# Attention scores as pairs of 64-row matmuls, with queries and keys loaded once and query tiles taken two at a time

## The chip, the cores and the metric

One NeuronCore of a Trainium2 chip runs the whole program. Its engines work side by side, each on its own queue: PE (TensorE, matmuls, with its weight loads, PEld, beside them), DVE (VectorE), ACT (ScalarE), POOL (GpSimd) and SP (SyncE), of which SP and POOL also issue the DMA transfers. The metric is the device time of one execution in microseconds. Differences of about 1% are the smallest that a measurement of this kernel tells from no change.

## What is computed

A two-layer decoder step in fp32, for a prompt of 2048 tokens and 32 sample tokens. Each layer projects its input, runs a branch (a state-space scan in layer 0, windowed attention with ALiBi in layer 1), adds attention over 256 memory slots, gates both, projects back and normalises. The change touches the two attentions of the prompt. Cut to what matters:

```python
def mem_attention(q, mem_k, mem_v):              # 4 heads of 64, 256 memory slots, in both layers
    s = jnp.einsum('bthe,bmhe->bhtm', q, mem_k).astype(jnp.float32) * SCALE
    p = jax.nn.softmax(s, axis=-1)
    o = jnp.einsum('bhtm,bmhe->bthe', p.astype(mem_v.dtype), mem_v)

def _dilated_group_full(q, k, v, slopes, window, dil):   # 3 groups (128,1), (512,4), (2048,16), 4 heads each
    # inside each residue stream: blocks of n=128 queries against (previous block, current block) of keys
    s = jnp.einsum('brjihe,brjuhe->brjhiu', qb, kb).astype(f32) * SCALE + bias
    s = jnp.where(valid[:, None], s, NEG_INF)
    lse = jax.nn.logsumexp(s, axis=-1)
    p = jnp.exp(s - lse[..., None])
    o = jnp.einsum('brjhiu,brjuhe->brjihe', p.astype(vb.dtype), vb)
```

## The kernel before

Every fp32 matmul whose precision matters is made of fp32r parts: a value is split into a high and a low part (`split`, L121: the high part by ACT, the low one by DVE). A projection is three matmuls, high x high, high x low and low x high (`mm3`, L126 to L130). The projections fill PE nearly all the time; the rows of the profile show them as `mm<-XH,wh` and the like. `XH` and `XL` are the split input, loaded from DRAM through `xraw`; `wh`, `wl` and `v` are split weights.

Beside the projections runs a side chain, written as a Python generator. The main loop calls `tick` after each three matmuls; `tick` advances the generator by one step (up to its next `yield`) for every so much projection work (`self.R` holds the rates). So the side chain's instructions are laid between the projections' in the order of the program, and a scheduler that knows when operands will be there settles the order on each engine. The attentions are parts of this side chain: `mem_attention` once in layer 0 (at 480 to 610 us of the profiled execution) and once in layer 1 (957 to 1150 us), `dilated` three times in layer 1, once for each group (from 1195, 1425 and 1635 us), with `dil_sample` after each.

Both attentions work on tiles of 128 queries and on two heads at a time, in blocks of four tiles:

- `load` brings queries (and, in `dilated`, keys) of one block from DRAM by POOL's queue into `qraw` or `raw`. One buffer holds one head: its 64 rows are read twice, into both halves of the 128 partitions (the `[0, 2]` in the access pattern, L915, L1541, L1542).
- `prep` makes `qs`, whose upper 64 partitions hold the high part of the scaled queries and whose lower ones the low part (ACT L927 or L1559, then DVE on 64 partitions, L928 or L1560), and splits the keys into `kh` and `kl` on both halves. In the memory attention `KH` and `KL` are made once.
- `st1` makes the scores of one tile: for each head one matmul with `kh` and one with `kl`, over 128 rows that hold the high and the low part of the queries, into `s` in PSUM (L938 and L939, L1579 and L1580); `s` has two buffers. In `mem_attention` DVE takes the extremum (`nm`, L941), ACT the exponential out of `s` (L945), DVE and POOL scale by the inverse sum (L950). In `dilated` DVE adds the bias, writes `P` and takes the extremum (`st`, L1583), and ACT takes the exponential in place (L1585).
- `st2` transposes `P` on PE (L959, L1595), and ACT and DVE in turn copy the result out to `PT` (`copy_out`, L132).
- `st3` multiplies with the values into `o`, 64 columns of the array for each head (L971, L1609; each fp32 matmul is two instructions in the trace). After the fourth tile of a block `o` is copied out to `ct` or `oT` and the same buffer serves the next block.

A step of the generator holds `st1` of tile n, then, after the `yield`, `st3` of tile n-4 and `st2` of tile n-2. In `dilated` the first group has three buffers of `raw`, the others four, two of which make a block; `qraw` has four. Nine steps pass between the first loads and the first `prep` of a `dilated`.

Of the kernel before, what the change touches and what calls it, by code (L numbers as in the profile page):

```python
# [13 lines left out]
OP = mybir.AluOpType  # L14
# [45 lines left out]
class Trunk:  # L60
# [827 lines left out]
    def mem_attention(self, l, d, side):  # L888
# [3 lines left out]
        with self.pool("ma", side=side) as p, self.pool("maps", space=PSUM, side=side) as psum:  # L892
            KH = p.tile([128, 4, 256], F32R, name="KH")
            KL = p.tile([128, 4, 256], F32R, name="KL")
            V = p.tile([128, 2, 256], F32, name="V")
            self.q2.dma_start(V, d["mv"][l].rearrange("(m p) t -> p m t", p=128))
            kd = []
            for h in range(0, 4, 2):
                raw = p.tile([128, 512], F32, name="qraw", bufs=4)
                for x in range(2):  # L900
                    self.q2.dma_start(raw[x * 64:x * 64 + 64].rearrange("p (h t) -> p h t", h=2),
                                      d["mk"][l, h * 64:h * 64 + 128].rearrange("(h e) t -> e h t", e=64))
                kd.append(raw.rearrange("p (h t) -> p h t", h=2))
# [6 lines left out]
            def load(j):  # L910
                ht, c0 = at(j)
                raws[j] = []
                for h in range(2):
                    raw = p.tile([128, 512], F32, name="qraw", bufs=4)
                    self.q2.dma_start(raw, dview(d["mq"], (ht * 2 + h) * 64 * NT + c0, [[0, 2], [NT, 64], [1, 512]]))  # L915
                    raws[j].append(raw)
# [6 lines left out]
            def prep(j):  # L923
                QS[j] = []
                for raw in raws.pop(j):
                    qs = p.tile([128, 512], F32R, name="qs", bufs=4)
                    nc.scalar.activation(qs, raw, AF.Copy, scale=-0.125)  # L927
                    v.scalar_tensor_tensor(qs[64:128], raw[64:128], -0.125, qs[64:128].bitcast(F32),  # L928
                                           op0=OP.mult, op1=OP.subtract)
                    QS[j].append(qs)  # L930

            def st1(n):
                j, t = divmod(n, 4)
                ht = at(j)[0]
                ts = slice(t * 128, t * 128 + 128)
                s = psum.tile([128, 2, 256], F32, name="s", bufs=2)
                for h in range(2):
                    mm(s[:, h], QS[j][h][:, ts], KH[:, ht * 2 + h], start=True, stop=False)  # L938
                    mm(s[:, h], QS[j][h][:, ts], KL[:, ht * 2 + h], start=False, stop=True)  # L939
                nm = p.tile([128, 2], F32, name="nm", bufs=4)  # L940
                v.tensor_reduce(nm, s, axis=AX.X, op=OP.min)  # L941
                P = p.tile([128, 2, 256], F32, name="P", bufs=3)
                sm = p.tile([128, 2], F32, name="sm", bufs=4)
                for h in range(2):
                    nc.scalar.activation(P[:, h], s[:, h], AF.Exp, scale=-1.0, bias=nm[:, h:h + 1],  # L945
                                         accum_out=sm[:, h:h + 1])
                rs = p.tile([128, 2], F32, name="rs", bufs=4)
                v.reciprocal(rs, sm)
                for h, eng in enumerate((v, nc.gpsimd if l == 0 else v)):
                    eng.tensor_scalar(P[:, h], P[:, h], rs[:, h:h + 1], None, op0=OP.mult)  # L950
                PP[n] = P

            def st2(n):
                P = PP.pop(n)
                tp = psum.tile([128, 2, 2, 128], F32, name="tp", bufs=2)
                PT[n] = p.tile([128, 2, 2, 128], F32, name="PT", bufs=3)
                for h in range(2):
                    for k in range(2):
                        nc.tensor.transpose(tp[:, h, k], P[:, h, k * 128:k * 128 + 128], ident)  # L959
                self.copy_out(PT[n], tp)  # L960

            def st3(n):
                j, t = divmod(n, 4)
# [3 lines left out]
                o, pt = O[j], PT.pop(n)  # L967
                for k in range(2):
                    for h in range(2):
                        c = (ht * 2 + h) * 64  # L970
                        mm(o[h * 64:h * 64 + 64, t * 128:t * 128 + 128], V[:, k, c:c + 64], pt[:, h, k],  # L971
                           start=k == 0, stop=k == 1)
                if t < 3:
                    return
# [8 lines left out]
            for h in range(2):  # L983
                self.split(KH[:, h * 2:h * 2 + 2], KL[:, h * 2:h * 2 + 2], kd[h])
            load(1)
            yield
# [3 lines left out]
            for n in range(36):  # L990
                if l == 0 and n == 8:
                    yield from self.wait("mg0")
                if n < 32:
                    st1(n)
                if n % 4 == 0 and n < 24:
                    load(n // 4 + 2)
                if l == 0 and n % 4 == 0 and n < 32:
                    load_gate(n // 4)
                if n % 4 == 2 and n < 28:
                    prep(n // 4 + 1)  # L1000
                yield
                if n >= 4:
                    st3(n - 4)
# [1157 lines left out]
```

## Time and profile before

| | us |
|---|---|
| median of 3 runs | 2058.67 |
| lowest and highest | 2046.83, 2061.18 |
| the profiled execution | 2061.28 |
| its span, first to last instruction | 2059.5 |

The profile is of one execution. An engine's busy time says how long it worked, and its idle time is put down to what ended it. A matmul's duration in the trace is from its issue to its modelled end; matmuls are pipelined, so that the distance from one start to the next, not the duration, is what one costs PE. PE's clock is given as the share of full speed that was granted in a stretch.

### The profile page before, as it was taken

The numbers are of one execution on the slowest core, as the hardware profiler recorded it, in microseconds if no ns is written. First come the engines' busy times: TensorE is split into PE (matmuls) and PEld (weight loads), VectorE is DVE, ScalarE is ACT, GpSimd is POOL, SyncE is SP. The second block draws the span as 40 slices with busy tenths as digits, with TensorE's granted clock in tenths as the row PEclk, the third lists the DMA queues.
The fourth block names the chain that finished last, engine by engine and source line by source line (L and its number), as shares of the span: only waits on it lengthen the run. The fifth ranks groups of instructions, "written<-read, shape, count | busy, mean of one in ns | idle before, by whom it ended". The sixth has DMA issues, their size and how long they took to land.

```text
span 2059.5 us, 35000 instructions
## 1 busy us (share of the span) xinstructions
PE 1943.8 (94%) x12806; PEld 1652.1 (80%) x12806; DVE 1235.8 (60%) x2888; ACT 722.7 (35%) x1651; POOL 490.5 (24%) x824
## 2 busy tenths in 40 slices
PE   8999999899899999998999988998899989999998
PEld 6789888788789887877888877797778767888777
DVE  8649989875676666663665146523652256454675
ACT  5333222424553311142454136522661256231010
POOL 0414444215430022211100122022302321311220
PEclk9999999999999999999999999999999989999999
DMA  7685655657659899876443496638958876858951
GB/s 223 188 225 139 186 176 178 207 167 224 179 161 271 281 347 368 293 237 174 117 142 100 143 197 172 165 101 189 208 148 234 200 166 188 274 167 246 278 164 72
DMA packets 473381, 406.56 MB, mean 197 GB/s; under 512 B 158264, under 2 KB 414696, under 8 KB 469928
## 3 DMA queue, kind: packets, MB, share of 16 engines
q1 hardware_dynamic: 384472, 257.52, 44.3%
q0 software_dynamic: 88736, 146.79, 24.0%
q8 instruction: 101, 1.65, 0.3%
q14 instruction: 72, 0.59, 0.1%
HBM read 297.99 MB, written 150.27 MB: 218 GB/s over the span
## 4 chain that ended last, share of the span: by engine, by line
PE 63%; DMA 19%; DVE 7%; issue 4%; ACT 2%; SPq 2%; POOL 2%; DVEq 0%; POOLq 0%; ACTq 0%
PE mm L128 17%; PE mm L129 16%; PE mm L130 16%; DMA raw<-e_kT 4%; DMA ot<-e_oT 2%; PE o L971 2%; DMA bcraw<-in_ssm_bc 2%; PE tp L959 2%; PE o L1609 2%; PE tp L1595 1%; DMA xraw<-d_x1TB 1%; DMA xraw<-in_xT 1%; DMA wraw<-in_w_in 1%; DMA xraw<-d_x1TA 1%; DMA wraw<-in_w_kv 1%
## 5 line engine op out<-in xcount | busy, mean ns | idle before, releaser
L128 PE MATMUL mm<-XH,wh 128*128 128x512 f32 (+2 forms) x1520 | 547.2, 361 | 23.9 <-DVE us L1391 8.3
L129 PE MATMUL mm<-XH,wl 128*128 128x512 f32 (+2 forms) x1520 | 543.3, 358 | 1.0 <-DVE wl L124 1.0
L130 PE MATMUL mm<-XL,wh 128*128 128x512 f32 (+2 forms) x1520 | 542.3, 358 | 1.4 <-DVE XL L124 1.4
L128 PEld LDWEIGHTS mm<-XH,wh 128*128 128x128 f32 x1520 | 290.2, 191 | 65.7 <-DVE us L1391 8.5
L130 PEld LDWEIGHTS mm<-XL,wh 128*128 128x128 f32 x1520 | 290.1, 191 | 43.2 <-DVE XL L124 2.9
L129 PEld LDWEIGHTS mm<-XH,wl 128*128 128x128 f32 x1520 | 289.6, 191 | 39.4 <-issue 2.6
L129 PE MATMUL mm<-WOH,cl 128*128 128x512 f32 (+1 forms) x512 | 198.6, 388 | 7.4 <-DVE cl L124 7.4
L128 PE MATMUL mm<-WOH,ch 128*128 128x512 f32 (+1 forms) x512 | 200.0, 392 | 0.4 <-ACT ch L123 0.4
L130 PE MATMUL mm<-WOL,ch 128*128 128x512 f32 (+1 forms) x512 | 198.7, 388 | 0.0
L124 DVE TENSOR_TENSOR XL<-xraw,XH 128x512 fp32r<-128x512 f32 (+2 forms) x176 | 99.7, 595 | 60.7 <-ACT XH L123 60.5
L124 DVE TENSOR_TENSOR wl<-wraw,wh 128x1024 fp32r<-128x1024 f32 (+1 forms) x87 | 103.6, 1191 | 48.6 <-ACT wh L123 47.8
L123 ACT ACTIVATE XH<-xraw 128x512 fp32r<-128x512 f32 (+2 forms) x176 | 92.5, 553 | 82.0 <-DMA xraw<-d_x1TB 27.3
L129 PEld LDWEIGHTS mm<-WOH,cl 128*128 128x128 f32 x512 | 96.8, 189 | 29.6 <-DVE cl L124 9.3
L128 PE MATMUL mm<-v,XH 128*128 128x256 f32 (+1 forms) x408 | 117.9, 289 | 0.2 <-DVE s L138 0.2
L130 PE MATMUL mm<-v,XH 128*128 128x256 f32 (+1 forms) x408 | 116.2, 285 | 0.0
L129 PE MATMUL mm<-v,XL 128*128 128x256 f32 (+1 forms) x408 | 116.0, 284 | 0.0
L130 PEld LDWEIGHTS mm<-WOL,ch 128*128 128x128 f32 x512 | 96.8, 189 | 21.3
L128 PEld LDWEIGHTS mm<-WOH,ch 128*128 128x128 f32 x512 | 96.6, 189 | 20.9 <-ACT ch L123 0.8
L1585 ACT ACTIVATE P<-P,st 128x128 f32<-128x128 f32 (+1 forms) x192 | 86.4, 452 | 48.4 <-DVE st L1583 48.2
L123 ACT ACTIVATE wh<-wraw 128x1024 fp32r<-128x1024 f32 (+1 forms) x87 | 89.2, 1026 | 22.0 <-PE mm L130 10.9
L1967 POOL COPY pace<-mark 1x1 f32<-1x1 f32 x88 | 31.4, 357 | 252.6 <-DVE mark L1966 229.2
L291 DVE SCALAR_TENSOR_TENSOR s<-s,mm 128x512 f32<-128x512 f32 (+2 forms) x80 | 46.8, 585 | 67.2 <-ACT s L290 61.2
(399 smaller groups left out, 3887.3 us busy)
## 6 DMA issues: line engine op xcount, KB each, us to landing
out_n_cache_dil_kv<-in_cache_dil_kv POOLq DMA_DIRECT2D x64, 512.0 KB, 6.1
wraw<-in_w_in SPq DMA_DIRECT2D x63, 512.0 KB
xraw<-d_x1TA SPq DMA_DIRECT2D x48, 256.0 KB
wraw<-in_w_kv SPq DMA_DIRECT2D x24, 512.0 KB
raw<-e_qT POOLq DMA_DIRECT2D x48, 256.0 KB, 12.4
xraw<-in_xT SPq DMA_DIRECT2D x40, 256.0 KB
raw<-e_kT POOLq DMA_DIRECT2D x36, 256.0 KB, 13.2
kv<-in_c_kT POOLq DMA_DIRECT2D x18, 512.0 KB, 5.7
```

Of the source, the lines that this page charges most:

```text
L123: self.nc.scalar.activation(hi, src, AF.Copy)
L124: self.nc.vector.tensor_tensor(lo, src, hi.bitcast(F32), op=OP.subtract)
L128: mm(out, wh, xh, start=first, stop=False)
L129: mm(out, wl, xh, start=False, stop=False)
L130: mm(out, wh, xl, start=False, stop=last)
L291: nc.vector.scalar_tensor_tensor(s[:, :n], s[:, :n], 1.0, p[:, :n], op0=OP.add, op1=OP.mult)
L959: nc.tensor.transpose(tp[:, h, k], P[:, h, k * 128:k * 128 + 128], ident)
L971: mm(o[h * 64:h * 64 + 64, t * 128:t * 128 + 128], V[:, k, c:c + 64], pt[:, h, k], start=k == 0, stop=k == 1)
L1585: nc.scalar.activation(P[:, h, lo:], P[:, h, lo:], AF.Exp, scale=-1.0, bias=at(0, hh, T), accum_out=at(1, hh, T))
L1595: nc.tensor.transpose(tp[:, h, k], P[:, h, k * 128:k * 128 + 128], ident)
L1609: mm(o[h * 64:h * 64 + 64, t * 128:t * 128 + 128], V[j][:, T - 1 + k - k0, h * 64:h * 64 + 64], pt[:, h, k], start=k == lo, stop=k == 1)
L1967: self.nc.gpsimd.tensor_copy(self.pace, mark)
```

## The change

The scores of both attentions are made differently, and the tiles go through the steps in pairs.

- Queries and keys of a block are loaded once for both heads, 128 plain rows (head 0 in partitions 0 to 63, head 1 in 64 to 127), into one buffer. There are three buffers, each of a whole block; in `dilated` three blocks are loaded at the start, and later ones after the keys of an earlier block were split.
- `prep` makes `qh` and `ql`, both on all 128 partitions (`split_q`), and `kh` and `kl` once for both heads. In `dilated` it is done in two parts, queries in one step and keys in the other.
- The new `scores` makes four products for each head, high and low queries with high and low keys. Each matmul has 64 rows, head 0's in the upper half of the array and head 1's in the lower (`tile_position`), one after the other.
- `st1`, `st2` and `st3` take two tiles at once. `s` now holds both, four banks' halves in one buffer instead of two buffers of one tile; `P` and `PT` have two buffers of a pair each.
- A turn of the loop has two steps: `st3` of pair m-3 and `st1` of pair m, a `yield`, then `prep` and `st2` of pair m-1. Six steps instead of nine pass between the first loads and the first `prep` of a `dilated`.

The core of the diff (`mem_attention` and `dilated` are changed alike):

```diff
             def load(j):
                 ht, c0 = at(j)
-                raws[j] = []
-                for h in range(2):
-                    raw = p.tile([128, 512], F32, name="qraw", bufs=4)
-                    self.q2.dma_start(raw, dview(d["mq"], (ht * 2 + h) * 64 * NT + c0, [[0, 2], [NT, 64], [1, 512]]))
-                    raws[j].append(raw)
+                raws[j] = p.tile([128, 512], F32, name="qraw", bufs=3)
+                self.q2.dma_start(raws[j], d["mq"][ht * 128:ht * 128 + 128, c0:c0 + 512])
...
-                s = psum.tile([128, 2, 256], F32, name="s", bufs=2)
-                for h in range(2):
-                    mm(s[:, h], QS[j][h][:, ts], KH[:, ht * 2 + h], start=True, stop=False)
-                    mm(s[:, h], QS[j][h][:, ts], KL[:, ht * 2 + h], start=False, stop=True)
+                s = psum.tile([128, 2, 2, 256], F32, name="s", bufs=1)
+                for y in range(2):
+                    ts = slice((t * 2 + y) * 128, (t * 2 + y) * 128 + 128)
+                    self.scores(s[:, :, y], QS[j], (KH[:, ht], KL[:, ht]), ts)
...
+    def split_q(self, qh, ql, raw):
+
+        self.nc.scalar.activation(qh, raw, AF.Copy, scale=-0.125)
+        self.nc.vector.scalar_tensor_tensor(ql, raw, -0.125, qh.bitcast(F32), op0=OP.mult, op1=OP.subtract)
+
+    def scores(self, s, q, k, ts, ks=slice(None)):
+
+        n = 0
+        for a in q:
+            for b in k:
+                for h in range(2):
+                    pp = slice(h * 64, h * 64 + 64)
+                    self.nc.tensor.matmul(s[:, h], a[pp, ts], b[pp, ks], start=n == 0, stop=n == 3, tile_position=(h * 64, 0))
+                n += 1
...
-            r = (c * 2 + h) * 64 * NT
-            raw = p.tile([128, 512 + W], F32, name="raw", bufs=4 if g else 3)
-            self.q2.dma_start(raw[:, 0:512], dview(d["qT"], r + qd * 512, [[0, 2], [NT, 64], [1, 512]]))
-            self.q2.dma_start(raw[:, 512:512 + n], dview(d["kT"], r + k0 * 128, [[0, 2], [NT, 64], [1, n]]))
-            RAW.setdefault(j, []).append(raw)
+            raw = p.tile([128, 512 + W], F32, name="raw", bufs=3)
+            rows = slice(c * 128, c * 128 + 128)
+            self.q2.dma_start(raw[:, 0:512], d["qT"][rows, qd * 512:qd * 512 + 512])
+            self.q2.dma_start(raw[:, 512:512 + n], d["kT"][rows, k0 * 128:k0 * 128 + n])
+            RAW[j] = raw
...
-        for n in range(36):
-            if n < 32:
-                st1(n)
-            if 1 <= n % 4 <= 2 and n < 28:
-                prep(n // 4 + 1, n % 4 - 1)
-            if n % 4 < 2 and n < 24:
-                load(n // 4 + 2, n % 4)
-            yield
-            if n >= 4:
-                st3(n - 4)
-            if 2 <= n <= 33:
-                st2(n - 2)
-            if n % 4 == 3 and n < 28:
-                load_v(n // 4 + 1)
+
+        for m in range(19):
+            j, t = divmod(m, 2)
+            if m >= 3:
+                st3(m - 3)
+            if m < 16:
+                st1(m)
+            if t == 0 and 0 < j < 8:
+                load_v(j)
+            yield
+            if j < 7:
+                prep(j + 1, t)
+                if t == 1 and j < 4:
+                    load(j + 4)
+            if 1 <= m <= 16:
+                st2(m - 1)
+            yield
```

How this moves instructions is shown at two places. The first is PE's queue in the first `dilated`, in its middle; L128 to L130 are projections of values, of which 21 stand between the groups. Before, one tile's step:

```order
L130 MATMUL mm<-v,XH_10075 128x256
L1609 MATMUL o<-PT,V 64x128 x4
L1595 MATMUL tp<-ident,P 128x128 x4
L1579 MATMUL s<-kh,qs 128x256
L1580 MATMUL s<-kl,qs 128x256
L1579 MATMUL s<-kh,qs 128x256
L1580 MATMUL s<-kl,qs 128x256
L128 MATMUL mm<-v,XH_10077 128x256
```

After, the two half-steps of a pair (the lines of the changed program are other ones: L1605 is the transpose, L1620 the output, L1014 the scores):

```order
L130 MATMUL mm<-v,XH_10041 128x256
L1605 MATMUL tp<-ident,P 128x128 x8
L128 MATMUL mm<-v,XH_10043 128x256
...
L130 MATMUL mm<-v,XH_10039 128x256
L1620 MATMUL o<-PT,V 64x128 x6
L1014 MATMUL s<-kh,qh 128x256 x2
L1014 MATMUL s<-kl,qh 128x256 x2
L1014 MATMUL s<-kh,ql 128x256 x2
L1014 MATMUL s<-kl,ql 128x256 x2
```

The rows of the scores stand twice, once for each tile of the pair. The outputs, which stood ahead of the transposes in each tile's step, now stand ahead of the scores, and the transposes stand alone between projections.

The second place is DVE's queue at the start of the first `dilated`, from the first split of keys to the first reader of scores (L1583, `ISA`). Before:

```order
L124 TENSOR_TENSOR kl<-raw,kh 128x512
L1560 SCALAR_TENSOR_TENSOR qs<-raw,qs 64x512
L124 TENSOR_TENSOR kl<-raw,kh 128x512
L1560 SCALAR_TENSOR_TENSOR qs<-raw,qs 64x512
L124 TENSOR_TENSOR wl<-wraw,wh 128x1024
L124 TENSOR_TENSOR kl<-raw,kh 128x640
L1560 SCALAR_TENSOR_TENSOR qs<-raw,qs 64x512
L124 TENSOR_TENSOR kl<-raw,kh 128x640
L138 COPY row<-mm 128x2x256
L1583 ISA P,st<-s,NB 128x128
```

After:

```order
L1005 SCALAR_TENSOR_TENSOR ql<-raw,qh 128x512
L124 TENSOR_TENSOR kl<-raw,kh 128x512
L1005 SCALAR_TENSOR_TENSOR ql<-raw,qh 128x512
L124 TENSOR_TENSOR kl<-raw,kh 128x640
L124 TENSOR_TENSOR wl<-wraw,wh 128x1024
L1592 ISA P,st<-s,NB 128x128
```

In both programs the splits of the second block (128x640) stand ahead of the first reader of scores; there are half as many of them.

## Rows read from the trace of the kernel before

**Rows 1.** The page's first lines: span, busy time and share by engine.

```profile
span 2059.5 us, 35000 instructions
PE 1943.8 (94%) x12806; PEld 1652.1 (80%) x12806; DVE 1235.8 (60%) x2888; ACT 722.7 (35%) x1651; POOL 490.5 (24%) x824
```

**Rows 2.** Windows of the three `dilated`: length, PE, PEld, DVE, ACT, POOL, clock, DMA.

```profile
1195.00:1360.00 165.00, 141.99 (x1051) 124.40 (x1050) 86.25 (x227) 86.80 (x225) 26.53 (x33) 0.94 0.70 165
1425.00:1550.00 125.00, 110.44 (x806) 91.75 (x804) 76.89 (x212) 76.79 (x213) 26.64 (x34) 0.95 0.82 184
1635.00:1750.00 115.00, 102.46 (x588) 79.57 (x588) 68.21 (x213) 68.79 (x213) 26.30 (x34) 0.93 0.75 179
```

**Rows 3.** Waits of PE, whole span: total us, times, longest us.

```profile
PE s L1579 <- ACT kh L123: 11.6, 3, 5.5
PE o L1609 <- ACT PT L136: 10.8, 4, 4.9
PE tp L1595 <- ACT P L1585: 10.6, 4, 5.6
PE s L1579 <- DVE st L1583: 8.0, 1, 8.0
...
PE o L1609 <- DVE PT L138: 3.6, 1, 3.6
PE o L1609 <- ACT oT L136: 3.5, 2, 1.8
```

**Rows 4.** Timeline of the first `dilated`: start, us, engine, line, [idle before <-releaser].

```profile
1207.00 0.79 POOL L1541 DMA_DIRECT2D raw<-e_qT  x1 [4.19 <-DVE kl L124]
...
1210.21 0.63 ACT L1559 ACTIVATE qs<-raw 128x512 fp32r<-128x512 f32 x1 [4.88 <-DMA raw<-e_qT]
...
1214.73 0.58 PE L1579 MATMUL s<-kh,qs 128*128 128x256 f32 x1 [8.04 <-DVE st L1583]
```

**Rows 5.** Timeline at the start of the second `dilated`.

```profile
1416.92 0.81 POOL L1542 DMA_DIRECT2D raw<-e_kT  x1
...
1430.45 0.63 ACT L123 ACTIVATE kh<-raw 128x512 fp32r<-128x512 f32 x1 [1.97 <-DMA raw<-e_kT]
...
1431.13 0.80 PE L1579 MATMUL s<-kh,qs 128*128 128x128 f32 x2 [5.54 <-ACT kh L123]
```

**Rows 6.** DMA issues of POOL's queue: count, KB each, median us to landing.

```profile
raw<-e_qT POOLq DMA_DIRECT2D x48, 256.0 KB, 12.4
...
raw<-e_kT POOLq DMA_DIRECT2D x36, 256.0 KB, 13.2
...
mg<-d_mg POOLq DMA_DIRECT2D x8, 256.0 KB, 7.2
```

**Rows 7.** Timeline of PE in the memory attention of layer 0.

```profile
499.80 0.28 PE L938 MATMUL s<-KH,qs 128*128 128x256 f32 x1
499.92 0.28 PE L939 MATMUL s<-KL,qs 128*128 128x256 f32 x1
...
501.20 0.40 PE L128 MATMUL mm<-XH,wh 128*128 128x512 f32 x1
501.53 0.66 PE L971 MATMUL o<-PT,V 128*64 128x128 f32 x8
502.12 0.44 PE L959 MATMUL tp<-ident,P 128*128 128x128 f32 x2
502.31 0.37 PE L938 MATMUL s<-KH,qs 128*128 128x256 f32 x1
...
516.62 0.60 PE L959 MATMUL tp<-ident,P 128*128 128x128 f32 x4
```

**Rows 8.** Groups by line and shape: count, busy us, mean ns, idle before.

```profile
L945 ACT ACTIVATE P<-s,nm 128x256 f32<-128x256 f32 x128 | 59.3, 470 | 54.9 <-DVE nm L941 52.7 <-PE tp L959 1.9
L941 DVE TENSOR_REDUCE nm<-s 128x2 f32<-128x512 f32 x64 | 43.6, 684 | 17.1 <-PE s L939 16.9
L1583 DVE CUSTOM_DVE_ANT_0 P<-s,NB 128x256 f32<-128x256 f32 x108 | 41.2, 419 | 16.5 <-PE s L1580 14.6 <-ACT P L1585 1.6
L1560 DVE SCALAR_TENSOR_TENSOR qs<-raw,qs 64x512 fp32r<-64x512 f32 x48 | 33.1, 690 | 42.1 <-ACT qs L1559 41.0
```

**Rows 9.** Timeline of ACT in the first `dilated`.

```profile
1258.34 0.63 ACT L123 ACTIVATE XH<-xraw 128x512 fp32r<-128x512 f32 x1 [6.97 <-DMA xraw<-d_x1TB]
```

## What was predicted before the change was run

> **What bounds the kernel now.** I read the page's first lines first: TensorE (PE) is busy for 1943.8 of 2059.5 us, so only what changes PE's work, its idle time or its clock can move the end [rows 1]. I then cut out the three stretches in which the windowed attention (`dilated`) runs beside the projections. There PE is busy for 141.99 of 165, 110.44 of 125 and 102.46 of 115 us: 23.0 + 14.6 + 12.5 = 50.1 us idle, with granted clocks of 0.94, 0.95 and 0.93 [rows 2]. The list of what PE waited for names five causes that make 48.1 us, nearly all of this: a key operand `kh` 11.6, `PT` (the transposed weights, copied out by ACT or DVE) 10.8 + 3.6, `P` 10.6, `st` 8.0 and `oT` 3.5 [rows 3]. The reader should see that all are ends of the attention's side chain, not of the projections.
>
> Behind them stand late loads of queries and keys. At 1207 us POOL could issue a query load only after DVE had read the buffer's last content (4.19 us idle). The load landed 3 us later; ACT had stood 4.88 us before `qs`, with the exponentials behind it on its queue, and DVE's readers of `s` stood behind the split, so PE waited 8.04 us for a score buffer [rows 4]. At the start of the second stage a key load issued at 1416.92 let ACT begin only at 1430.45, and PE had waited 5.54 us [rows 5]. These loads read 64 rows twice, to fill both halves: the keys' land in 13.2 us, the queries' in 12.4; a load of the same 256 KB in plain rows, `mg`, lands in 7.2 [rows 6].
>
> **The change, part by part.**
>
> *Scores.* Before, 640 score matmuls (128 + 128 of the memory attention, 192 + 192 of the windowed one) are issued 0.12 us apart at 256 columns (499.80, 499.92) [rows 7]: 640 x 0.12 = 77 us. After, 1280 matmuls stand in 640 pairs that use different halves of the array's rows. No row shows two row halves at work together. The nearest row is the output matmul on 64 columns of the array: eight of them take 0.66 us, where four transposes over the same 128 columns take 0.60 [rows 7]. With a tail of 0.27 us in both, the transposes are (0.60 - 0.27)/3 = 0.11 us apart and the outputs (0.66 - 0.27)/7 = 0.056, so two column halves do run side by side, their weight loads with them. Bounds: 0 us if a pair costs what one matmul did, +77 us if the halves take turns; no gain is possible, as each half still streams the same 256 columns four times. I take 0, by the nearest row.
>
> *Changes of array mode.* From the matmul at 501.20 to the score at 502.31 pass 1.11 us; without a change of mode they would be 0.23 + 8 x 0.056 + 0.12 = 0.80 (the steps of the main matmul, the outputs, the transposes), so one trip into 64 columns and back costs 0.3 us, 0.15 a change [rows 7]. By the order of instructions there are 305 such changes around outputs now, and 321 around outputs and scores after: the pair halves the trips for outputs, the scores add their own. That is 16 x 0.15 = +2.4 us; 163 of them enter or leave the row mode, which no row prices, and at double they would give +24 more. I take +5. The Trainium skill (TensorEngine Tiling (Array Packing), section Tiling Modes) says that changing the mode drains TensorE while tiles of one mode load and multiply in parallel; the 0.3 us agrees with the first half, the 0.056 us with the second, and no row here shows it for rows of the array. By the row's 0.15 us the sum holds +2.4 us; by the rule each of the 163 drains as well, which is the same +2.4 as long as a drain of the row mode costs what a drain of the column mode does.
>
> *Splits and loads.* Per block of four tiles one query split and one key split replace two each, on full partitions; 48 DVE operations of 690 ns on half the partitions become 24 [rows 8]. DVE and ACT are busy for little over half of these stretches [rows 2], so I price it at nothing; covered by PE's own work, it shows only through the waits below. The halved load count lets three whole blocks be in flight where one and a half (first stage) or two were. In PE's order a later block's operands are then loaded some five pairs ahead. So `st` (8.0) and `P` (10.6), which rest on ACT standing before a late `raw`, should go: -18.6 us; bound below, 0, if the loads are not what is late. At the second stage's start PE's order is unchanged, with the same 67 projection matmuls ahead of the first score, so the 11.6 us for `kh` stay except that plain rows land sooner: 13.2 against 7.2 us, up to 6 us at each of two starts. I take -7 [rows 3, 6].
>
> *Pairs of tiles.* The transposes of a pair and its outputs stand three half-steps apart, where they stood two steps apart, and the output buffer is reused after a pair instead of a tile: -3 for `oT`. `PT` (14.4) has another source too: at 1258.34 ACT had stood 6.97 us before a projection operand (`XH`, from DRAM), with the exponentials behind it [rows 9]. The change only lightens the traffic there. I take -5 of 14.4, bounds 0 and -14.
>
> *One score buffer.* `s` now holds a pair, once, where it held two tiles. The next pair's scores wait until the last reader is done: in the windowed stages four reductions, 4 x 0.42 = 1.7 us; in the memory attention one reduction over twice the columns, up to 2 x 0.68, and four exponentials of 0.47, 3.3 us [rows 8]. PE has between two pairs, by the order, some 21 matmuls twice and eight transposes: 42 x 0.12 + 8 x 0.11 = 5.9 us. So it waits when ACT or DVE start late by 2.6 to 4.2 us. Standing of that size remains where projection operands are late [rows 9]: a wait of about 3 us each, and where the memory attention meets the gated unit's first matmuls. I take +8, bounds 0 and +40 (half of the 80 pairs, 1 us each). Behind a waiting score stand the projection matmuls on PE, and ACT's and DVE's next readers then have nothing to read.
>
> *Clock.* (1 - clock) x length over the three stretches is 9.9 + 6.3 + 8.0 = 24 us of lost speed at most (half at the low level of the two, 1.2 against 2.4 GHz, part of it idle time anyway) [rows 2]. PE stands before the drops (5.54 us, ended at 1431.13, in a stretch of 0.95) [rows 5]. With about half of the idle time gone I take a third back: -8.
>
> Sum: 0 + 5 - 18.6 - 7 - 3 - 5 + 8 - 8 = -28.6 us. The profiled execution took 2061.28 us (span 2059.5 and 1.8 around it); 2061.3 - 28.6 = 2032.7. The median of the runs, 2058.67, lies 2.6 lower: **2030 us**.
>
> **Rivals.**
> - *The halves take turns* (slower). For it: no row shows row halves together. Against: the column halves do. Price 77 us from the first pair on: 2030 + 77 = 2107. It decides as soon as a pair is issued more than about 0.23 us after the last instead of 0.12.
> - *The single score buffer binds.* For: ACT and DVE stand up to 7 us before operands [rows 9]. Against: 5.9 us between pairs. At its upper bound, 40 instead of 8: 2062, no change.
> - *Row mode is dear.* For it stands only that no row shows it. With 0.3 us for each of the 163 changes into and out of it: 2030 + 24 = 2054. The Trainium skill's rule on draining would act through this.
> - *The change does not do what it says*: operands were late because of the traffic or POOL's queue, not because of buffers; then the loads stay late and only the +5 and +8 are left: 2059 + 13 = 2072. Against it: POOL's idle time ended by DVE [rows 4].
> - *More goes than I take*: all 50 us and two thirds of the clock's 24: 2059 + 5 - 50 - 16 = 1998.
>
> **Chances.** My forecast, with its own range 2015 to 2045: 0.45 (0.33 of it faster by over 1%, that is under 2038; about 1% is what a measurement of this kernel can tell from no change). Halves in turn 0.14, slower. Score buffer 0.12, no change for 0.09, slower 0.03. Dear row mode 0.08, no change. Not what it says 0.06, no change for 0.04, slower 0.02. More goes: 0.15, faster. Faster 0.33 + 0.15 = 0.48; within 1% (2038 to 2079) 0.12 + 0.09 + 0.08 + 0.04 = 0.33; slower 0.14 + 0.03 + 0.02 = 0.19. The range 1998 to 2080 leaves out the halves in turn and little else.
>
> **What will show it.** Two score matmuls of a pair must start almost together, the next pair 0.12 us later; at 0.23 us my first term is wrong. `qh` and `kh` should no longer wait for `raw` inside a stage, only at its start, and `raw` should land in 7 to 9 us. PE's waits for `st` and `P` should be gone; a wait of scores for DVE or ACT readers of `s`, summed over stages, is the price of the single buffer: above 20 us my sum is off. The granted clock of the three stages should rise to 0.96 or more.

## The result and the profile after

The changed kernel takes 1988.66 us (median of 4 runs) where the kernel before, beside it, took 2059.93: a ratio of 0.967 (95% interval 0.962 to 0.972). It is 3.3% faster, 41 us less than the 2030 us forecast and 9 us below the range. The profiled execution took 1987.37 us, against 2061.28 before: 73.9 us less. Of the four executions of the run with three products (below) one took 4348.43 us, without a known cause; its median is of all four (1968.18 without that one), its ratio of the other three.

The page's first lines after, which answer to [rows 1]:

```profile
span 1985.6 us, 35812 instructions
PE 1933.8 (97%) x13446; PEld 1649.3 (83%) x13446; DVE 1177.6 (59%) x2758; ACT 687.6 (35%) x1585; POOL 419.0 (21%) x754
```

PE is idle for 51.8 us where it was for 115.7: 63.9 us of the gain are idle time. The other 10 us are PE's busy time; PE got a mean clock of 0.991 of full speed instead of 0.978.

Windows of the kernel after: length, then busy time of PE, PEld, DVE, ACT and POOL, granted clock, DMA share, GB/s. First the second memory attention, then the three windowed ones, which answer to [rows 2]:

```profile
966.00:1137.00 171.00, 171.00 (x1379) 149.76 (x1378) 92.49 (x178) 75.93 (x202) 6.52 (x12) 1.00 0.35 109
1186.00:1336.00 150.00, 150.00 (x1313) 134.92 (x1311) 75.25 (x212) 76.60 (x209) 9.45 (x14) 1.00 0.49 149
1360.00:1504.00 144.00, 144.00 (x1213) 121.85 (x1212) 72.90 (x212) 74.14 (x208) 17.18 (x28) 1.00 0.61 170
1572.00:1692.00 120.00, 119.48 (x811) 93.12 (x810) 60.72 (x209) 64.70 (x209) 10.77 (x18) 1.00 0.49 155
```

In the windowed attentions 50.1 us of idle time have become 0.5, and the clock is 1.00 throughout, where it was 0.93 to 0.95.

PE's waits in the whole span after, total us, times, longest; they answer to [rows 3]:

```profile
PE mm L128 <- ACT wh L123: 7.4, 3, 5.9
PE s L1014 <- ACT P L934: 5.9, 2, 5.2
...
PE o L963 <- ACT PT L136: 0.5, 1, 0.5
...
PE tp L1605 <- ACT P L1594: 0.4, 1, 0.4
```

Of the five causes in [rows 3] the windowed attentions keep 0.4 us, a wait for `P` (L1605); the 0.5 us of L963 are of a memory attention. The wait that grew most is that of scores for the single buffer (`s` L1014 for the exponentials of L934), 5.9 us where it was 0.4, both times in the first memory attention.

Loads on POOL's queue after: count, KB each, median us to landing; they answer to [rows 6]:

```profile
raw<-e_qT POOLq DMA_DIRECT2D x24, 256.0 KB, 4.1
raw<-e_kT POOLq DMA_DIRECT2D x18, 256.0 KB, 5.4
V<-e_V POOLq DMA_DIRECT2D x18, 256.0 KB, 3.8
qraw<-d_mq POOLq DMA_DIRECT2D x8, 256.0 KB, 4.4
mg<-d_mg POOLq DMA_DIRECT2D x8, 256.0 KB, 4.9
```

Queries land in 4.1 us, where they took 12.4. What surprises is `mg`: its code did not change, and its median went from 7.2 to 4.9. Something in the old loads had held up the loads behind them as well.

PE in the first windowed attention after, a pair's outputs and scores (a row merges neighbours of one kind; x2 are the two heads):

```profile
1242.73 1.09 PE L1620 MATMUL o<-PT,V 128*64 128x128 f32 x16
1243.76 0.39 PE L1014 MATMUL s<-kh,qh 64*128 64x256 f32 x2
1243.98 0.28 PE L1014 MATMUL s<-kl,qh 64*128 64x256 f32 x2
1244.09 0.28 PE L1014 MATMUL s<-kh,ql 64*128 64x256 f32 x2
1244.21 0.28 PE L1014 MATMUL s<-kl,ql 64*128 64x256 f32 x2
1244.33 0.28 PE L1014 MATMUL s<-kh,qh 64*128 64x256 f32 x2
...
1244.69 0.28 PE L1014 MATMUL s<-kl,ql 64*128 64x256 f32 x2
1244.90 0.50 PE L128 MATMUL mm<-XH,wh 128*128 128x512 f32 x1
```

The pairs stand 0.12 us apart, as the single matmuls did in [rows 7]; the two of a pair start 1 to 5 ns apart in this run (3 ns in the median of all 640 pairs). So the two row halves work at once.

### The profile page after: what moved, and what is told of

Read it like the earlier page. It is cut to its first block, busy times and chain, and to the rows that moved or that the text cites. A ratio compares the mean times of both kernels' runs of the same rounds, so it can differ in the third digit from the quotient of the medians.

```text
span 1985.6 us, 35812 instructions
## 1 busy us (share of the span) xinstructions
PE 1933.8 (97%) x13446; PEld 1649.3 (83%) x13446; DVE 1177.6 (59%) x2758; ACT 687.6 (35%) x1585; POOL 419.0 (21%) x754
## 4 chain that ended last, share of the span: by engine, by line
PE 77%; DVE 9%; DMA 8%; issue 2%; POOL 2%; SPq 1%; ACT 1%; DVEq 0%; POOLq 0%; ACTq 0%
PE mm L128 20%; PE mm L129 20%; PE mm L130 20%; PE s L1014 4%; PE o L1620 2%; PE tp L1605 2%; DMA bcraw<-in_ssm_bc 2%; PE o L963 2%; DMA ot<-e_oT 2%; PE tp L950 1%; DMA xraw<-in_xT 1%; DVE wl L124 1%; DVE H L675 1%; PE tp L1366 1%; DMA craw<-d_cm 1%
## 5 line engine op out<-in xcount | busy, mean ns | idle before, releaser
L128 PE MATMUL mm<-XH,wh 128*128 128x512 f32 (+2 forms) x1520 | 546.9, 360 | 13.8 <-ACT wh L123 7.4
L130 PE MATMUL mm<-XL,wh 128*128 128x512 f32 (+2 forms) x1520 | 538.2, 355 | 1.5 <-DVE XL L124 1.4
L128 PEld LDWEIGHTS mm<-XH,wh 128*128 128x128 f32 x1520 | 287.5, 189 | 60.8 <-ACT wh L123 8.0
L130 PEld LDWEIGHTS mm<-XL,wh 128*128 128x128 f32 x1520 | 287.3, 189 | 44.7 <-DVE XL L124 4.1
L128 PE MATMUL mm<-WOH,ch 128*128 128x512 f32 (+1 forms) x512 | 199.6, 391 | 0.5 <-ACT ch L123 0.5
L130 PE MATMUL mm<-WOL,ch 128*128 128x512 f32 (+1 forms) x512 | 198.8, 388 | 0.0
L128 PE MATMUL mm<-v,XH 128*128 128x256 f32 (+1 forms) x408 | 118.0, 289 | 0.0
L130 PE MATMUL mm<-v,XH 128*128 128x256 f32 (+1 forms) x408 | 115.4, 283 | 0.0
L130 PEld LDWEIGHTS mm<-WOL,ch 128*128 128x128 f32 x512 | 96.6, 189 | 21.3
L128 PEld LDWEIGHTS mm<-WOH,ch 128*128 128x128 f32 x512 | 96.6, 189 | 21.0 <-ACT ch L123 0.9
L123 ACT ACTIVATE wh<-wraw 128x1024 fp32r<-128x1024 f32 (+1 forms) x87 | 89.3, 1027 | 23.6 <-DMA wraw<-in_w_in 10.2
L1592 DVE CUSTOM_DVE_ANT_0 P<-s,NB 128x128 f32<-128x128 f32 (+1 forms) x192 | 58.7, 362 | 60.3 <-PE s L1014 60.0
```

Source lines behind the costliest of these rows:

```text
L123: self.nc.scalar.activation(hi, src, AF.Copy)
L128: mm(out, wh, xh, start=first, stop=False)
L130: mm(out, wh, xl, start=False, stop=last)
L1592: v.tensor_tensor_reduce(out=P[:, h, y, lo:], in0=s[:, h, y, lo:], in1=NB[hp][:, h, lo:], scale=1.0, scalar=3e38, op0=OP.add, op1=OP.min, ...
```

## Experiments

Three theories stood against each other. **Theory 1**: the form of the old loads, 64 rows read twice, is what was late. **Theory 2**: too few blocks were in flight. **Theory 3**: tiles in pairs gave the side chain its slack.

### The kernel before, with plain loads of 64 rows

```diff
-            self.q2.dma_start(raw[:, 0:512], dview(d["qT"], r + qd * 512, [[0, 2], [NT, 64], [1, 512]]))
-            self.q2.dma_start(raw[:, 512:512 + n], dview(d["kT"], r + k0 * 128, [[0, 2], [NT, 64], [1, n]]))
+            for x in range(2):
+                xx = slice(x * 64, x * 64 + 64)
+                self.q2.dma_start(raw[xx, 0:512], dview(d["qT"], r + qd * 512, [[NT, 64], [1, 512]]))
+                self.q2.dma_start(raw[xx, 512:512 + n], dview(d["kT"], r + k0 * 128, [[NT, 64], [1, n]]))
```

(and the same for `qraw`)

> The kernel before, with one edit: each load of queries or keys that read 64 rows twice is issued as two plain loads of 64 rows, one for each half of the partitions; same bytes, same buffers, twice as many issues. Theory 1 (the form of the load is what is late: the form that reads twice lands 8 us later than plain rows and holds up what stands behind it on POOL's queue): the loads land in 4 to 6 us, PE's 50 us of idle time in the three windowed attentions falls below 15, the 8 us wait at the start of the second memory attention shrinks too, time 2000 to 2015. Theory 2 (too few blocks in flight) and theory 3 (tiles not in pairs): idle time stays at 40 or more, 2045 to 2065.

Measured: 1982.26 us, ratio to the kernel before 0.960 (0.957 to 0.964), below even the 2000 to 2015 of theory 1. This one edit gives the whole gain of the change; its interval overlaps with the changed kernel's. Its windowed attentions:

```profile
1183.00:1340.00 157.00, 153.86 (x1202) 136.31 (x1201) 87.36 (x231) 86.08 (x225) 36.92 (x68) 0.99 0.68 176
1385.00:1500.00 115.00, 115.00 (x854) 96.99 (x853) 77.30 (x213) 74.93 (x211) 35.28 (x65) 1.00 0.79 205
1575.00:1685.00 110.00, 110.00 (x666) 88.54 (x665) 71.57 (x225) 71.56 (x221) 33.80 (x62) 1.00 0.73 201
```

3.1 us of idle time are left of 50.1, with the same bytes, the same buffers, the same order of tiles and the old score matmuls. The DMA engines are as busy as they were (a share of 0.68 to 0.79, before 0.70 to 0.82), so it wasn't the amount of traffic that made the loads late. Its loads on POOL's queue:

```profile
raw<-e_qT POOLq DMA_DIRECT2D x96, 128.0 KB, 5.7
...
raw<-e_kT POOLq DMA_DIRECT2D x72, 128.0 KB, 4.9
...
V<-e_V POOLq DMA_DIRECT2D x18, 256.0 KB, 4.4
```

Twice as many issues, each of half the bytes, and each lands in less than half the time; `V`, untouched, lands in 4.4 instead of 8.8 us. So theory 1 holds in that the form of the loads was what was late, and for the time theories 2 and 3 aren't needed.

### The same edit in the memory attentions only

> The kernel before with plain loads of 64 rows in the two memory attentions only; the windowed ones keep loads that read twice. Theory 1 (the form of the load): only what waits in the memory attentions goes, which is the 8.3 us at their second start and some 3 us in the first one: 2045 to 2053. If the lighter queue helps beyond its own stage: below 2040.

Measured: 2047.34 us, ratio 0.994 (0.992 to 0.996). The 8.3 us idle at the second memory attention's start are gone (window 957 to 1150 us: PE busy for all 193.00 us), and the windowed attentions keep their waits (`tp` for `P` 9.4, `o` for `PT` 9.0, `s` for `kh` 8.6, `s` for `st` 7.8). Each stage pays for its own loads; most of the gain, some 67 of 82 us, lies in the windowed ones.

### The changed kernel with the old loads

```diff
-            raw = p.tile([128, 512 + W], F32, name="raw", bufs=3)
-            self.q2.dma_start(raw[:, 0:512], d["qT"][rows, qd * 512:qd * 512 + 512])
+            raw = p.tile([128, 512 + W], F32, name="raw", bufs=4 if g else 3)
+            self.q2.dma_start(raw[:, 0:512], dview(d["qT"], r + qd * 512, [[0, 2], [NT, 64], [1, 512]]))
...
+                for h in range(2):
+                    pp = slice(h * 64, h * 64 + 64)
+                    self.split_q(q[0][pp], q[1][pp], raw[h][pp, 0:512])
```

> The changed kernel with the loads of the kernel before: one buffer for each head, its 64 rows read twice into both halves, as few buffers as before (4, in the first windowed attention 3); of each buffer the half that is needed is split, in operations on 64 partitions, two for each one. Pairs and row halves stay. Theories 1 and 2 (form of the loads, blocks in flight): the waits of before come back, 2025 to 2045. Theory 3 (it was the pairs that gave the side chain its slack): within 1% of the changed kernel, 1985 to 2005.

Measured: 2094.94 us, 1.4% slower than the kernel before (1.009 to 1.018): worse than theories 1 and 2 said. Its largest waits of PE:

```profile
PE s L1019 <- DVE st L1601: 21.3, 6, 6.8
PE s L1019 <- ACT kh L123: 15.3, 3, 6.8
PE s L1019 <- ACT P L939: 11.3, 1, 11.3
PE tp L1614 <- ACT PT L136: 10.3, 2, 7.5
```

21.3 + 11.3 us are scores that wait for readers of the one score buffer. So the rival "the single score buffer binds" is real: with late loads it costs 33 us, with plain ones 5.9. In this run, with the old loads, pairs and row halves made the kernel slower.

### The changed kernel with two blocks in flight

```diff
-            raw = p.tile([128, 512 + W], F32, name="raw", bufs=3)
+            raw = p.tile([128, 512 + W], F32, name="raw", bufs=2)
...
-                if t == 1 and j < 4:
-                    load(j + 4)
+                if t == 1 and j < 5:
+                    load(j + 3)
```

> The changed kernel with two buffers of queries and keys instead of three in the windowed attentions: two blocks in flight, each load issued as late as before. Theory 2 (blocks in flight): 2005 to 2030. Theories 1 and 3: no change, 1983 to 1995, since a plain load lands in 4 us and its block is wanted some 15 us after the issue.

Measured: 1986.23 us, ratio 0.962 (0.959 to 0.965), the changed kernel's time. With plain loads the third buffer is worth nothing. Theory 2 falls as the cause of the gain.

### What in the old form is slow

The old pattern has three steps, `[0, 2], [NT, 64], [1, 512]`: two blocks, 64 rows, 512 columns, and the distance between the blocks is zero. Two runs of the changed kernel were made to take that apart. The first writes its plain loads as two blocks with a distance of 64 rows, so that they are 128 even rows after all:

```diff
-                self.q2.dma_start(raws[j], d["mq"][ht * 128:ht * 128 + 128, c0:c0 + 512])
+                self.q2.dma_start(raws[j], dview(d["mq"], ht * 128 * NT + c0, [[64 * NT, 2], [NT, 64], [1, 512]]))
```

> The changed kernel with its loads of queries and keys written as two blocks of 64 rows (a pattern of three steps, like the one before, but with the distance of 64 rows where that one had zero): the same rows to the same places. If reading the same rows twice makes the load late: no change, 1983 to 1995, no packets of 8 bytes. If the three-step pattern does: loads land 8 us later and packets of 8 bytes appear, 2030 to 2095, as with the old loads.

Measured: 1990.83 us, ratio 0.965 (0.962 to 0.968): no change. But the run separates nothing: as built, its loads have the pattern `[NT, 128], [1, 512]`, the same two steps as the changed kernel's, so it is that kernel once more. What speaks against three steps as such is `V`: its pattern, `[256, 128], [32768, n // 128], [1, 128]`, has three steps with 128 entries outermost, and its 256 KB land in 3.8 us in the changed kernel. The second run sets the blocks 128 rows apart, and as built its loads keep three steps with two entries outermost:

```diff
-                self.q2.dma_start(raws[j], d["mq"][ht * 128:ht * 128 + 128, c0:c0 + 512])
+                self.q2.dma_start(raws[j], dview(d["mq"], ht * 64 * NT + c0, [[128 * NT, 2], [NT, 64], [1, 512]]))
```

> The changed kernel with the two blocks of 64 rows of each load taken 128 rows apart (heads 0 and 2, or 1 and 3, instead of 0 and 1; only the loads are changed, so heads are computed with values of another pair): no row is read twice, but the pattern cannot be written as 128 even rows. Theory Z (reading the same rows twice is what is slow): no change, 1983 to 1995. Theory O (what is slow is a pattern whose outermost step has only two entries: then two of the 16 DMA engines carry the load, 32 packets of 4096 bytes each, and the other 14 get 32 packets of 8 bytes each, which makes the 448 seen per load): such packets appear, loads land in 8 to 14 us instead of 3 to 5, 2030 to 2095.

Measured: 2026.38 us, ratio 0.983 (0.979 to 0.986), 38 us over the changed kernel and just under theory O's range. Its loads:

```profile
raw<-e_qT POOLq DMA_DIRECT2D x24, 256.0 KB, 10.6
...
raw<-e_kT POOLq DMA_DIRECT2D x18, 256.0 KB, 11.5
```

No row is read twice, and the loads are nearly as late as the old ones (12.4 and 13.2). So it isn't the reading twice; with `V` beside it, it is an outermost step with only two entries. The DMA records show how. Counted by size, POOL's queue moved these packets:

```
                        8 bytes   4096 bytes
before                   57,344       20,048
after                         0       16,208
before, plain halves          0       20,048
after, old loads         57,344       19,920
after, blocks apart      28,672       16,208
```

The kernel before has 128 such loads (32 of `qraw`, 96 of `raw`), the run with blocks apart 64: 448 packets of 8 bytes for each load, which is 14 x 32, beside the 64 = 2 x 32 of 4096 bytes that hold 256 KB (of 5120 bytes where a load has 640 columns). That is what 2 of 16 engines at work and 14 with empty packets would leave. In time it shows where little else runs. The first window is of the kernel before, whose two `qraw` loads issued at 531.0 and 531.9 (median landing 8.9 us) are then in flight, with a store and `mg` issued behind them. For 3.0 us in all, between 533 and 541, exactly four packets of 4096 bytes are on the engines at once, which fits two for each load:

```profile
538.00:543.00 5.00, 5.00 (x41) 3.91 (x38) 3.59 (x7) 3.24 (x11) 1.16 (x2) 1.00 0.23 88
```

The other is of the kernel after, with one plain `qraw` load of the same 256 KB, issued at 511.8 and landed 3.0 us later, and the transfers behind it:

```profile
512.00:516.00 4.00, 4.00 (x19) 3.24 (x18) 3.40 (x8) 2.40 (x7) 3.36 (x5) 1.00 0.60 160
```

0.23 of 16 engines are 3.7, at 88 GB/s; the plain load gets 0.60 and 160 GB/s together with its neighbours. That it is 2 engines is worked out from the packets, since the records don't name the engine; that the outermost step of two decides is shown by the run with blocks apart beside `V`.

### Steps of one tile

> The changed kernel with the windowed attentions in steps of one tile in the order of before (scores of tile n; outputs of n-4 and transposes of n-2); loads, row halves and the one buffer of scores for two tiles stay. Theory 3 (pairs): the waits for PT, oT and P come back, 15 to 30 us, 2003 to 2020. Theories 1 and 2: 1985 to 2000, the upper end if scores wait for their one buffer or the changes of array mode double (about 100 more, 0.15 us each).

```diff
-                s = psum.tile([128, 2, 2, 256], F32, name="s", bufs=1)
...
+            if n % 2 == 0:
+                SS[0] = psum.tile([128, 2, 2, 256], F32, name="s", bufs=1)
+            s = SS[0][:, :, n % 2]
```

Measured: 2086.18 us, ratio 1.010 (1.007 to 1.014), far from either expectation, and it doesn't tell what it was made for. Windows of its third windowed attention and of what comes behind:

```profile
1648.00:1806.00 158.00, 157.45 (x1065) 124.75 (x1064) 66.15 (x220) 70.55 (x217) 9.36 (x15) 1.00 0.38 121
1806.00:1880.00 74.00, 35.38 (x365) 27.09 (x363) 23.73 (x53) 8.98 (x14) 27.60 (x41) 0.70 0.64 201
```

PE hardly waits inside the attention (157.45 of 158 us busy). But the attention is spread over 615 projection matmuls where the changed kernel has 300 between the third attention's first and last score: one tile for some 19 of them, where the changed kernel puts a pair. The projections are nearly used up, and the sampling attention behind it runs nearly uncovered, 35.38 of 74 us busy at a clock of 0.70. That single tiles with one score buffer made the scheduler spread them so is a reading, not shown.

Of the 102 us between the two profiled executions 56 are idle time, 39 of them in this last window. The other 46 are PE's busy time, and here the run does say what pairs are worth. From start to next start, gaps left out, scores, outputs and transposes of the windowed attentions (the scores with those of the memory attentions, which are alike) take 194.9 us where the changed kernel takes 167.0, and PE changes its array mode 402 times in these stretches instead of 200: 28 us, 0.14 for each change more. So with row halves, steps of one tile cost about 28 us of PE's time by themselves. Whether pairs also give the side chain slack (theory 3) stays open.

### Row halves in another order

First four products of head 0, then four of head 1:

```diff
-        for a in q:
-            for b in k:
-                for h in range(2):
+        for h in range(2):
+            pp = slice(h * 64, h * 64 + 64)
+            for a in q:
+                for b in k:
```

> The changed kernel with the score matmuls of a tile in another order: four products of head 0, then four of head 1, so that neighbours use the same half of the array's rows. Theory A (row halves work side by side, which makes the scores cost nothing more than before): a tile's eight matmuls take 8 x 0.118 us instead of 4 x 0.118, 160 tiles of 0.47 us make 75 us, 2055 to 2070. Theory B (the order doesn't matter, a 64-row matmul is itself only half as long): 1985 to 1995.

Measured: 1993.99 us, ratio 0.967 (0.964 to 0.970): no 75 us. Theory A's 75 us fell, but theory B's reason isn't it either, since a half's matmuls still stand 0.12 us apart. In PE's queue, as built, four matmuls of head 0 stand ahead of four of head 1, and yet the trace shows them in twos, 0.12 us from two to two:

```profile
1245.34 0.40 PE L1014 MATMUL s<-kh,qh 64*128 64x256 f32 x2
1245.56 0.29 PE L1014 MATMUL s<-kl,qh 64*128 64x256 f32 x2
1245.68 0.29 PE L1014 MATMUL s<-kh,ql 64*128 64x256 f32 x2
1245.80 0.28 PE L1014 MATMUL s<-kl,ql 64*128 64x256 f32 x2
```

Head 1's first matmul starts with head 0's first, ahead of three that stand before it in the queue. Eight and eight shows how far this goes:

```diff
-                for y in range(2):
+                for h, y in ((0, 0), (0, 1), (1, 0), (1, 1)):
...
-                    self.scores(s[:, :, y], QS[j], (KH[:, ht], KL[:, ht]), ts)
+                    self.scores(h, s[:, :, y], QS[j], (KH[:, ht], KL[:, ht]), ts)
```

(and the same in `dilated`; `scores` now makes the products of one head, and the scheduler keeps their order)

> The changed kernel with all eight score matmuls of head 0 of a pair of tiles ahead of the eight of head 1, kept in that order. In the run with four and four, matmuls of the two heads still started together, 16 of them took 1.25 us instead of 1.14. Theory A (each half of the rows takes its own matmuls as they come, far ahead of the other half): about the same again, 1.25 to 1.4 us for 16, 1990 to 2005. Theory B (only a few matmuls can run ahead): the second half of the sixteen starts late, 1.5 to 2.0 us for 16, 80 pairs, 2010 to 2060.

Measured: 2030.43 us, ratio 0.984 (0.981 to 0.987). Theory B holds:

```profile
1238.04 0.38 PE L1013 MATMUL s<-kh,qh 64*128 64x256 f32 x1
...
1238.50 0.28 PE L1013 MATMUL s<-kl,ql 64*128 64x256 f32 x1
1238.62 0.39 PE L1013 MATMUL s<-kh,qh 64*128 64x256 f32 x2
...
1238.97 0.39 PE L1013 MATMUL s<-kl,ql 64*128 64x256 f32 x2
1239.20 0.28 PE L1013 MATMUL s<-kh,qh 64*128 64x256 f32 x1
...
1239.56 0.28 PE L1013 MATMUL s<-kl,ql 64*128 64x256 f32 x1
```

Four of head 0 run alone, four of both heads together, four of head 1 alone. A pair of tiles takes 1.72 us instead of 1.14 (medians over 77 and 78 pairs); 80 pairs x 0.58 = 46 us, and the run is 42 us longer than the changed kernel. That agrees with the price of the first rival: with no overlap at all, eight more steps of 0.118 for each of 80 pairs would have cost 76 us.

### Three products instead of four

```diff
-        for a in q:
-            for b in k:
+        for a, b in ((q[0], k[0]), (q[0], k[1]), (q[1], k[0])):
```

> The changed kernel without the product of the low part of the queries with the low part of the keys (the projections leave out low x low too): six matmuls for each tile instead of eight. Theory A (a pair costs 0.118 us of PE): 160 pairs less, 19 us, 1965 to 1972, if PE stays the bound. Theory B (PE waits for the side chain instead): 1980 to 1990.

Measured: 1968.27 us, ratio 0.955 (0.951 to 0.959), faster than both kernels. 160 pairs x 0.118 = 19 us were expected of it, and 20.4 came. This is what the row halves can do and the old stacking could not: there the low and the high part of the queries shared one matmul, so that leaving out low x low would have left as many matmuls of 256 columns (by count; no run tried it).

## Why the prediction was wrong

**What bounds the kernel** was read rightly: the idle time in the windowed attentions, ended by late loads. It was worth more than was taken: 63.9 us of PE's idle time went, 25.6 were forecast (-18.6 - 7 - 3 - 5 + 8).

**Score pairs: 0.** Right, the pairs stand 0.12 us apart. **Changes of array mode: +5.** Right in sum. The plain-halves run has the old matmuls at nearly the new clock, so it is the one to compare with. From start to next start, gaps left out, scores take 91.0 us after against 87.4 there, outputs 78.8 against 85.0, transposes 62.8 against 55.2: +3.6 - 6.2 + 7.6 = +5.0. The prediction counted changes around outputs and scores alone, so that the dearer transposes in this sum make its agreement partly luck. Of a run of 16 score matmuls, 1.144 us are eight steps of 0.118 and 0.20 for the way into and out of the row mode, 0.10 each; the dear row mode did not come.

**`st` and `P`: -18.6.** Right in size (18.2 of it went), wrong in reason. The prediction put it down to three blocks in flight; with two blocks nothing changes, and with plain loads alone, at the old depth, it goes as well. The row that it rested on was misread: the load issued at 1207.00, after the wait for a buffer, is not the one that landed 3 us later. It landed after 16.4 us. What ended ACT's 4.88 us [rows 4] was a load issued 12.9 us earlier, at 1197.34:

```profile
L1541 POOL DMA_DIRECT2D raw<-e_qT x1: 838/838/838, 1197.3 to 1197.3; - x1
...
  ACT qs L1559: 4.9, 1
...
DMA to landing us min/median/max: 12.9/12.9/12.9
```

So already there it was the load's way that was long; its issue had waited 3.9 us for a buffer.

**`kh` at the stages' starts: -7.** All 11.6 went. The first failed step is the landing time, mis-sized: 7.2 us was taken for plain rows from `mg` [rows 6]. That median was itself made of loads stuck behind old ones: `mg` landed 8.6 and 10.0 us after the issues at 534.19 and 545.14, with old loads ahead of it, and 3.5 and 3.2 at 577.09 and 589.40, with no such load in flight. One row of the same form was taken as clean without asking what else was on the queue. Plain loads land in 4.1 to 5.4 us.

**`PT`: -5 of 14.4; `oT`: -3.** All of both went. Here stands the larger failed step. The prediction saw that ACT stood 6.97 us before a projection operand from SP's queue [rows 9], called it another source, and said that the change only lightened the traffic there. Of the 14.4 us, 9.7 follow such waits of ACT for `XH` (5.9, 7.0 and 5.5 us long), and 4.1 follow one of 12.3 us for weights from the same queue. ACT's waits for `XH` between 1180 and 1760 us before:

```profile
ACT XH L123 <- DMA xraw<-d_x1TB: 23.8, 10, 7.0
ACT XH L123 <- DMA xraw<-d_x1TA: 14.0, 3, 5.5
```

And after:

```profile
ACT XH L123 <- DMA xraw<-d_x1TB: 8.4, 8, 2.6
...
ACT XH L123 <- DMA xraw<-d_x1TA: 2.6, 2, 2.4
```

They make 37.8 us before, 11.0 after, 18.4 with plain halves, and 33.0 with blocks apart (up to 1800 us there). So half of it goes when nothing but the form of the loads is changed: it was in good part the same source. That loads which crowd a few DMA engines hold up transfers that are spread over all of them is the reading that fits; the waits are what was measured.

**What was not in the sum:** 8.3 us at the start of the second memory attention (`PE mm L128 <- DVE us L1391: 8.3, 1, 8.3` in the list of waits before), where a small query load (`sq`) stood right behind three old loads on POOL's queue. It landed 10.2 us after its issue; after the change, behind two plain loads, 4.2. The prediction had the wait's kind in view and did not count the queue.

**One score buffer: +8.** 5.9 us, where the memory attention meets the gated unit, as foreseen, and nothing in the windowed attentions. With old loads it is 33 us, inside the bound of 40.

**Clock: -8.** The projections' matmuls, gaps left out, take 1559.9 us instead of 1570.1: -10.2.

Some 11 us of smaller waits that went lie outside these places and were not traced further.

**The rivals.** "The change does not do what it says" held the right cause, traffic and POOL's queue instead of buffers, and drew the wrong end from it: that the loads stay late. The change replaces the very form that made the traffic. "More goes than I take" came, and its 1998 was 9 us too high, since it counted the windowed attentions alone. What would have given it from the trace before: `raw` took 12.4 to 13.2 us for the bytes that `mg` could get in 3.2 (the shortest of its landings). A difference of 9 us for the same 256 KB on the same queue asks for a reason, and the pattern in the code was the plainest thing that differed. The Trainium skill (DMA: Bandwidth & Descriptors, section Rules for kernel authors) states that reason: an outermost dimension of fewer than 16 entries, such as a leading broadcast of c copies, keeps the whole transfer to at most c engines. The packets and the run with blocks apart agree with it, and the prediction did not weigh it.

## What to carry to other kernels

Look at a load's landing time in proportion to its bytes before looking at how deep it is prefetched: one pattern whose outermost step has two entries cost this kernel 3 to 4%. Of PE's waits that went, some 30 us were for what these loads bring themselves (`kh`, `st`, `P`), and some 22 came through other transfers that waited behind or beside them (`PT`, `sq`). Two plain loads were better here than one that reads the same rows twice. When a change bundles several edits, try the smallest of them alone: here one edit of the kernel before gives 1982 us, and only with it in place does it show what the rest is worth (nothing by itself, 20 us once it lets a product be left out).

## What the runs showed of the hardware

A load of 256 KB on POOL's queue landed at the earliest 8.3 us after its issue with an outermost step of two, and 2.8 in plain rows; the slow form left 448 packets of 8 bytes for each load. While it was in use, operands from the other queue were late too (ACT's waits for `XH`: 37.8 us, 18.4 with nothing changed but the form of the loads).

Matmuls on the two halves of the array's rows overlap even when they don't alternate in the queue: one half ran up to four matmuls ahead of the queue's order, and in the run with eight no more (four and four: 1.25 us for 16 matmuls; eight and eight: 1.72; alternating: 1.14). So for two halves the order need not be exact, but eight of one head ahead of eight of the other cost time here. A change of array mode cost 0.14 us in the run with steps of one tile, by the 28 us of 202 more changes.
